# Nine gate and up pairs by seven block products, and activations split at the down projection

## The chip, the cores and the metric

The kernel runs on one NeuronCore of a Trainium2 chip. The metric is the device time of one execution in microseconds. TensorE (PE; its weight loads are PEld), VectorE (DVE), ScalarE (ACT) and GpSimd (POOL) each work off their own instructions in order; SyncE (SP) issues the DMAs. They wait for one another through semaphores.

## The reference

One block of a hybrid network on 512 tokens of width 1024 in float32: an SSD branch and a dilated attention branch are merged, and a feed-forward with a causal convolution follows. The change touches the last part:

```python
x = x + merged @ w_out[l]
h2 = rms_norm(x, norm2_g[l])
u = causal_dwconv(h2 @ w_up[l], ffn_conv_w[l], ffn_conv_b[l])   # 3 taps over tokens
u_gate, u_val = jnp.split(u, 2, axis=-1)                        # 2816 columns each
x = x + (jax.nn.silu(u_gate) * u_val) @ w_down[l]
```

## The kernel before

**Numbers.** Every matrix product is made of three matmuls: an operand `a` is split into `ahi` (a cast to fp32r, on ACT) and `alo` (`a - ahi`, on DVE), and `hi*hi + hi*lo + lo*hi` is summed in PSUM. `make_piece` (L100, L101) does so for each weight piece of 128 x 1024 elements (512 KB) that `load_piece` (L88, SP) brings; raw pieces have three buffers, their `whi` and `wlo` three each. `stt` (L52) is a helper for DVE's `scalar_tensor_tensor`.

**End of the merge.** `mm_tok` (L902) multiplies the merged activations by `w_out`, four 128-token blocks in four PSUM banks, two halves of 512 output columns (`ps_wo`). `add_x1` (L931, L933) adds the residual into `x1` in SBUF. Then the second norm: `second_norm` (L201, and `pow` on POOL in L202), `second_scale` (L52, tile `hn`), `second_t` (four transposes per half on PE, L208, and the cast `h2h` on ACT, L211), and the subtraction `h2l` on DVE (L212). Their order on DVE and ACT is written out by hand. The first gate and up pair is woven into it: its matmuls take 256 tokens at a time, so that they can begin while the last two token blocks are still normed.

**Feed-forward.** The 22 blocks `m` of 128 columns each have a gate and an up column block, together a pair. `mm_chan` (L140) makes 24 matmuls of 512 tokens for each of the two (8 slices of the width, 3 combinations). `conv3` reads the PSUM bank: ACT starts the sum (L1001), DVE adds two shifted taps (L52, tile `facc`). Gate: silu on ACT (L1022). Up: product on DVE (L1025), then the split for the down projection (L1026 on ACT, L1027 on DVE) into `act_h`, `act_l`, which stay in SBUF.

**Down projection.** `mm_tok` again (`ps_wd`), two halves of 512 columns, 11 pieces each; a piece is 24 matmuls of 512 columns. `store` adds `x1` and writes the output.

What orders DVE, ACT and POOL from the feed-forward on is the tile scheduler; PE's order is that of the code.

Of the kernel before, what the change touches and what calls it, by code (L numbers as in the profile page):

```python
# [38 lines left out]
def kernel(  # L39
# [856 lines left out]
    def mm_tok(xh, xl, nk, name, fin, last):
        pss = [bank("mm", f"ps_{name}{b}") for b in range(NT)]

        def part(b, k0, w):
            for j, (ww, xx) in enumerate(((w[0], xh), (w[0], xl), (w[1], xh))):  # L900
                for k in range(2):
                    nc.tensor.matmul(pss[b], xx[:, k0 + k, b * P:(b + 1) * P], ww[:, k, :],  # L902
                                     start=(k0 == 0 and j == 0 and k == 0),
                                     stop=(k0 == nk - 2 and j == 2 and k == 1))
# [43 lines left out]
    def second_t(b):  # L948
        for half in range(2):
            rest2[b, half] = transpose_half(hn2[b], b, half, "h", h2h, h2l)  # L950

    mm_tok(mh, ml, KD, "wo0_", lambda b, ps: add_x1(0, b, ps), 1)
    ending = mm_tok(mh, ml, KD, "wo1_", None, 2)
    with tc.manual_schedule(engines={mybir.EngineType.DVE, mybir.EngineType.Activation}):
        prefetch(1)
        add_x1(1, 0, ending(0))
        second_norm(0)
        second_scale(0, 0)
        add_x1(1, 1, ending(1))
        second_scale(0, 1)  # L960
        second_norm(1)
        second_scale(1, 0)
        ps = ending(2)
        second_t(0)
        add_x1(1, 2, ps)
        second_scale(1, 1)
        second_norm(2)
        rest2[0, 0]()
        rest2[0, 1]()
        second_scale(2, 0)  # L970
        ps = ending(3)
        second_t(1)
        add_x1(1, 3, ps)
        second_scale(2, 1)
        rest2[1, 0]()
        rest2[1, 1]()
        second_norm(3)
        up0 = [bank("mm", f"ps_u0_{i}") for i in range(2)]
        wu = [next_piece()]
        mm_chan(up0[0], wu[0], h2h, h2l, nt=256, ticks=False, lo_first=True)  # L980
        second_scale(3, 0)
        second_scale(3, 1)
        second_t(2)
        wu.append(next_piece(0))
        rest2[2, 0]()
        rest2[2, 1]()
        mm_chan(up0[1], wu[1], h2h, h2l, nt=256, ticks=False)
        prefetch(1)
        second_t(3)
        rest2[3, 0]()  # L990
        rest2[3, 1]()
        for i in range(2):
            mm_chan(up0[i], wu[i], h2h, h2l, t0=256, nt=256, ticks=False, lo_first=True)
# [74 lines left out]
```

## Time and profile before

| what | us |
|---|---|
| device time, median of 3 runs (1229.62 to 1232.95) | 1231.42 |
| device time of the profiled execution | 1231.49 |
| its span in the profile | 1229.8 |
| first gate and up matmul | 861.81 |
| first down matmul | 1106.27 |

A page of the profile has the busy time of each engine, the chain of work that ended last (followed back from the last instruction), and groups of equal instructions. Further views are the timeline of single instructions (start, duration, engine, line, operation, output <- inputs, and in brackets the idle time before it with what ended that), and the busy time in given stretches. A timeline row with x8 merges eight instructions that follow each other.

### The profile page before, as it was taken

How to read it: one execution, taken by the hardware profiler on the slowest of the kernel's cores; microseconds unless marked ns; L12 is line 12 of the kernel's file. 1: busy time of each engine (PE TensorE's matmuls, PEld its weight loads, DVE VectorE, ACT ScalarE, POOL GpSimd, SP SyncE). 2: the span in 40 equal slices, each digit the busy share in tenths (PEclk: the TensorE clock that was granted, in tenths of full speed). 3: DMA queues.
4: the chain of work that ended last, by engine and by line, in shares of the span. 5: the costliest groups of instructions: out<-in, count | busy, mean ns of one | idle time of the engine just before them, and what ended most of it. 6: DMA issues, size and time to landing. Idle time of an engine off the chain costs nothing.

```text
span 1229.8 us, 15236 instructions
## 1 busy us (share of the span) xinstructions
PE 1219.1 (99%) x6040; PEld 1021.0 (83%) x6040; DVE 701.0 (57%) x953; ACT 556.0 (45%) x847; POOL 94.4 (8%) x75
## 2 busy tenths in 40 slices
PE   9999999999999999999999999999999999999998
PEld 7889889898888788888888888888888888888887
DVE  6345544545789887777744354654765666653322
ACT  4344555747746656465433334433544444442210
POOL 1020202120001201101011000000000000000000
PEclk9999999999999999999999999999999999999999
DMA  5423222122645644434234422342333333232330
GB/s 183 120 69 92 57 64 69 54 78 61 184 124 150 166 130 121 127 87 137 70 74 129 140 87 102 103 172 85 103 88 102 96 93 103 87 102 92 107 127 34
DMA packets 152535, 128.12 MB, mean 104 GB/s; under 512 B 10368, under 2 KB 123632, under 8 KB 151441
## 3 DMA queue, kind: packets, MB, share of 16 engines
q1 hardware_dynamic: 152465, 127.16, 35.1%
q8 instruction: 47, 0.77, 0.3%
q14 instruction: 23, 0.19, 0.1%
HBM read 124.73 MB, written 2.41 MB: 103 GB/s over the span
## 4 chain that ended last, share of the span: by engine, by line
PE 91%; ACT 4%; DVE 3%; POOL 1%; issue 1%; POOLq 0%; ACTq 0%; DVEq 0%
PE ps_u L140 20%; PE ps_ssd L140 19%; PE ps_wd L902 10%; PE ps_qk L398 9%; PE ps_gate L140 7%; PE ps_sp L875 7%; PE ps_v L398 6%; PE ps_wo L902 4%; PE ps_ap L140 2%; ACT s L521 1%; PE ps_y L723 1%; PE ps_o L728 1%; PE ps_s L502 1%; POOL qrs L202 1%; PE ps_pv L540 1%; PE ps_st L704 1%
## 5 line engine op out<-in xcount | busy, mean ns | idle before, releaser
L101 DVE TENSOR_TENSOR wlo<-raw,whi 128x1024 fp32r<-128x1024 f32 x194 | 243.3, 1255 | 338.1 <-ACT whi L100 216.2
L100 ACT CAST whi<-raw 128x1024 fp32r<-128x1024 f32 x194 | 203.2, 1048 | 316.9 <-PE ps_wd L902 79.8
L140 PE MATMUL ps_ssd<-hl,whi 128*128 128x512 f32 x384 | 103.0, 397 | 0.0
L140 PE MATMUL ps_ssd<-hh,whi 128*128 128x512 f32 x384 | 98.2, 398 | 0.0
L140 PE MATMUL ps_ssd<-hh,wlo 128*128 128x512 f32 x384 | 95.3, 390 | 0.0
L140 PE MATMUL ps_u<-h2h,whi 128*128 128x512 f32 (+1 forms) x368 | 88.7, 383 | 0.3 <-ACT h2h L211 0.2
L140 PE MATMUL ps_u<-h2h,wlo 128*128 128x512 f32 (+1 forms) x368 | 88.1, 382 | 0.0
L140 PE MATMUL ps_u<-h2l,whi 128*128 128x512 f32 (+1 forms) x368 | 88.0, 382 | 0.0
L140 PEld LDWEIGHTS ps_ssd<-hh,wlo 128*128 128x128 f32 x384 | 72.1, 188 | 15.8
L140 PEld LDWEIGHTS ps_ssd<-hh,whi 128*128 128x128 f32 x384 | 70.9, 188 | 14.3
L140 PEld LDWEIGHTS ps_ssd<-hl,whi 128*128 128x128 f32 x384 | 70.1, 188 | 13.7 <-issue 0.6
L140 PEld LDWEIGHTS ps_u<-h2h,whi 128*128 128x128 f32 x368 | 67.2, 188 | 14.5 <-ACT h2h L211 0.8
L140 PEld LDWEIGHTS ps_u<-h2l,whi 128*128 128x128 f32 x368 | 67.2, 188 | 13.9
L140 PEld LDWEIGHTS ps_u<-h2h,wlo 128*128 128x128 f32 x368 | 67.2, 188 | 13.6
L52 DVE SCALAR_TENSOR_TENSOR facc<-ps_u,sc,facc 128x511 f32<-128x511 f32 x88 | 65.8, 747 | 5.8 <-ACT facc L1001 4.3
L398 PE MATMUL ps_qk<-whi,hh 128*128 128x512 f32 x192 | 66.9, 430 | 0.0
L398 PE MATMUL ps_qk<-whi,hl 128*128 128x512 f32 x192 | 60.3, 395 | 0.0
L398 PE MATMUL ps_qk<-wlo,hh 128*128 128x512 f32 x192 | 60.1, 395 | 0.0
L202 POOL TENSOR_TENSOR qrs<-qss,nhalf 128x8 f32<-128x8 f32 x24 | 44.0, 1833 | 170.7 <-DVE qss L201 170.7
L902 PE MATMUL ps_wd<-wlo,acth 128*128 128x512 f32 x176 | 54.3, 389 | 0.0
L902 PE MATMUL ps_wd<-whi,acth 128*128 128x512 f32 x176 | 54.2, 389 | 0.0
L902 PE MATMUL ps_wd<-whi,actl 128*128 128x512 f32 x176 | 54.2, 389 | 0.0
(238 smaller groups left out, 2057.9 us busy)
## 6 DMA issues: line engine op xcount, KB each, us to landing
raw<-in_w_in_dram SPq DMA_DIRECT2D x100, 512.0 KB
raw<-in_w_up_dram SPq DMA_DIRECT2D x44, 512.0 KB
raw<-in_w_down_dram SPq DMA_DIRECT2D x22, 512.0 KB
bc<-scr_a SPq DMA_DIRECT2D x8, 1024.0 KB
raw<-in_w_ssd_proj_dram SPq DMA_DIRECT2D x16, 512.0 KB
eb<-scr_e SPq DMA_DIRECT2D x16, 256.0 KB
raw<-in_w_out_dram SPq DMA_DIRECT2D x8, 512.0 KB
fb<-scr_f SPq DMA_DIRECT2D x24, 128.0 KB
```

What stands on the lines that cost most here:

```text
L52: nc.vector.scalar_tensor_tensor(o, a, s, b, op0=op0, op1=op1)
L100: nc.scalar.copy(hi, raw)
L101: nc.vector.tensor_sub(lo, raw, hi.bitcast(F32))
L140: nc.tensor.matmul(ps[:, t0:t0 + nt], a[:, k, c:c + n], b[:, k, t0:t0 + nt], start=(i == 0), stop=(i == total - 1))
L202: return nc.gpsimd.tensor_tensor(rs, ss, nhalf.broadcast_to(tuple(ss.shape)) if ss.shape[1] > 1 else nhalf, op=ALU.pow)
L398: nc.tensor.matmul(pss[b], tok(g, kq * 2 + k, b, xx), w[:, k, :], start=(kq == 0 and j == 0 and k == 0), stop=(kq == 3 and j == 2 and k == 1))
L502: nc.tensor.matmul(pss[h][:, o:o + nk * P], qt[hp, j, q * P:(q + 1) * P], kt[hp, j, (q - nk + 1) * P:(q + 1) * P], start=True, stop=True)
L521: nc.scalar.activation(s[:, o:o + nk * P], s[:, o:o + nk * P], AF.Exp, bias=st[:, q, 0, 2 * j + h:2 * j + h + 1], accum_out=st[:, q, 1, 2 ...
L540: nc.tensor.matmul(pso[h * 64:(h + 1) * 64, q * P:(q + 1) * P], vt[:, q - nk + 1 + kb, (2 * j + h) * 64:(2 * j + h + 1) * 64], pts[h][:, o ...
L704: nc.tensor.matmul(sts[c], btok[:, c, :], xdc[:, c].rearrange("p h d -> p (h d)"), start=True, stop=True)
L875: nc.tensor.matmul(pss[j], w[:, k, cs], ys[k][xi], start=(k2 == 0 and i == 0 and k == 0), stop=(k2 == 7 and i == 2 and k == 1))
L902: nc.tensor.matmul(pss[b], xx[:, k0 + k, b * P:(b + 1) * P], ww[:, k, :], start=(k0 == 0 and j == 0 and k == 0), stop=(k0 == nk - 2 and j ...
```

## The change

**Seven products for nine pairs.** The pairs 3, 5, ..., 19 are `fast`; the other 13 are taken as before. A fast pair regards the weights as a 2 x 2 block matrix (lower and upper half of the width; gate and up) and the activations as another (halves of the width; halves of the tokens), and forms the product with seven block products instead of eight, in Winograd's form of Strassen's algorithm. A block product is 12 matmuls of 256 tokens: 4 slices of the half width, 3 combinations.

- The sums of activations, S1 to S4 (each 128 x 1024), are made once, in the course of the first two pairs, on POOL and DVE, in space that `act` needs only later, and are split into `sh` and `sl`.
- The sums of weights, `t12` and `t34` (`form` 1 to 4, each 128 x 512), are made per fast pair on POOL. Such a pair then has three weight pieces to split and a half one (`w1`, `w2`, `w3`, `wb`) instead of two.
- The seven products land in four PSUM banks and are added on ACT and DVE (`sum_1`, `sum_2`, `sum_u`, `sum_g`) into `ua` and `ga` in SBUF, which the convolution reads.

**Order.** DVE, ACT and POOL have an order by hand through the whole feed-forward: the convolution of a pair runs beside the matmuls of the next one, and its weights are split one pair ahead.

**Activations are split later.** `act` stays in float32 (44 KB per partition). The down projection splits each block when it gets there (`ahead`, tiles `asp`, ten buffers), for each of its two halves anew; blocks 0 and 1 are split in the last pair. `x1` is written to DRAM after the second norm (`x1d`) and read again (`x1b`) for the final sum.

```diff
-    def mm_tok(xh, xl, nk, name, fin, last):
+    def mm_tok(xs, nk, name, fin, last, ahead=lambda k: None):
...
                 if b == 1:
+                    ahead(k0 + 2)
                     prefetch()
         ws = [next_piece(0) for i in range(last)]
+        for i in range(1, last):
+            ahead(nk - 2 * last + 2 * i)
...
+        if nh == 1:
+            nc.sync.dma_start(x1d[b * P:(b + 1) * P, :], x1[:, b, :])
...
+    PLAIN = (0, 1, *range(2, NF, 2), NF - 1)
...
+    def f_early():
+        nc.gpsimd.tensor_add(f11, h2h[quad(0, 0)].bitcast(F32), h2l[quad(0, 0)].bitcast(F32))
+        nc.gpsimd.tensor_add(f12, h2h[quad(1, 0)].bitcast(F32), h2l[quad(1, 0)].bitcast(F32))
...
+    def f_late(b):
+        for half, f in enumerate((f21, f22)):
+            nc.scalar.copy(f[:, :, (b - 2) * P:(b - 1) * P], tr2[b, half])
...
+        if which == 1:
+            nc.gpsimd.tensor_sub(w["t12"][lo_half(0)], u[lo_half(0)], g[lo_half(0)])
+        elif which == 2:
+            nc.gpsimd.tensor_sub(w["t12"][lo_half(1)], u[lo_half(1)], w["t12"][lo_half(0)])
+        elif which == 3:
+            nc.gpsimd.tensor_sub(w["t34"][lo_half(0)], u[lo_half(1)], u[lo_half(0)])
+        else:
+            nc.gpsimd.tensor_sub(w["t34"][lo_half(1)], g[lo_half(1)], w["t12"][lo_half(1)])
...
+    PRODUCTS = (("1", 0, "A11", "a", 0), ("1", 1, "A12", "c", 0), ("2", 0, "S1", "b", 1), ("2", 1, "S2", "a", 1),
+                ("3", 0, "S3", "b", 0), ("3", 1, "A22", "c", 1), ("b", 0, "S4", "d", 0))
...
+    def product(m, x, half, xo, bk, c):
...
+        for a, b in ((wh, xh), (wh, xl), (wl, xh)):
+            for k in range(4):
+                nc.tensor.matmul(ba[m][bk][:, c * H:(c + 1) * H], a[:, k, :], b[:, k, :],
+                                 start=(i == 0), stop=(i == 11))
...
+    def sum_1(m):
+        if fast(m):
+            tsum[m] = gu.tile([P, 3, H], F32, tag="ts", name=f"ts{m}", bufs=1)
+            nc.scalar.copy(tsum[m][:, 0], ba[m]["a"][:, :H])
...
+    def sum_2(m):
+        if fast(m):
+            t = tsum[m]
+            nc.vector.tensor_add(t[:, 1], t[:, 0], ba[m]["a"][:, H:])
+            nc.vector.tensor_add(t[:, 2], t[:, 1], ba[m]["b"][:, :H])
...
+            nc.vector.tensor_add(ua[m].rearrange("p (a t) -> p a t", a=2), tsum[m][:, 1:3],
+                                 ba[m]["b"][:, H:].unsqueeze(1).broadcast_to((P, 2, H)))
+            nc.vector.tensor_add(ua[m][:, :H], ua[m][:, :H], ba[m]["d"][:, :H])
...
+            nc.vector.tensor_add(ga[m].rearrange("p (a t) -> p a t", a=2), tsum[m][:, 0:3:2],
+                                 ba[m]["c"].rearrange("p (a t) -> p a t", a=2))
...
+    nc.vector.tensor_add(s1f, f21, f22)
+    nc.gpsimd.tensor_sub(s2f, s1f, f11)
+    nc.vector.tensor_sub(s3f, f11, f21)
...
+    nc.gpsimd.tensor_sub(s4f, f12, s2f)
...
+    def split_act(k, p, tag, bufs):
+        t = p.tile([P, 2, S], F32R, tag=tag, name=f"{tag}{len(asp)}_{k}", bufs=bufs)
+        nc.scalar.copy(t[:, 0, :], act[:, k, :])
+        nc.vector.tensor_sub(t[:, 1, :], act[:, k, :], t[:, 0, :].bitcast(F32))
+        return t
...
+        if fast(m):
+            steps[0]()
+            conv_a(m - 1, 1)
+            rest(m, "3")
+            load_up(m + 2)
+            steps[1]()
+            conv_a(m - 1, 0)
+            conv_s(m - 1, 1)
+            steps[2]()
+            cast(m + 1, "1")
+            rest(m, "b")
+            form(m + 2, 1)
+            steps[3]()
+            rest(m + 1, "1")
+            form(m + 2, 2)
+            steps[4]()
+            cast(m + 1, "3")
+            conv_s(m - 1, 0)
+            steps[5]()
+            silu_g(m - 1)
+            rest(m + 1, "3")
+            steps[6]()
+            mul(m - 1)
+            continue
...
+    mm_tok(xs_a, NF, "wd0_", store(0), 2, ahead)
+    ahead(0)
+    mm_tok(xs_a, NF, "wd1_", store(1), 2, ahead)
```

**The same in the instructions.** DVE in the middle of the feed-forward, before: one pair, the remainders of its two weight pieces, the convolution from PSUM (`ps_u`), the product and the split of the result.

```order
L101 TENSOR_TENSOR wlo141_7359<-raw141_7356,whi141_7358 128x1024
L52 SCALAR_TENSOR_TENSOR facc5_0_7339<-ps_u5_0_7307,sc_85,facc5_0_7339 128x511
L52 SCALAR_TENSOR_TENSOR facc5_0_7339<-ps_u5_0_7307,sc_85,facc5_0_7339 128x510
L101 TENSOR_TENSOR wlo142_7398<-raw142_7395,whi142_7397 128x1024
L52 SCALAR_TENSOR_TENSOR facc5_1_7374<-ps_u5_1_7308,sc_85,facc5_1_7374 128x511
L52 SCALAR_TENSOR_TENSOR facc5_1_7374<-ps_u5_1_7308,sc_85,facc5_1_7374 128x510
L1025 TENSOR_TENSOR facc5_1_7374<-facc5_1_7374,facc5_0_7339 128x512
L1027 TENSOR_TENSOR actl_6992<-facc5_1_7374,acth_6991 128x512
```

DVE there after the change, from the sums of the fast pair 11 (`ps_ua` to `ps_ud` are its four banks) to its product; `ulo1` and `ulo2` are remainders of pair 13.

```order
L1085 TENSOR_TENSOR ts11_8129<-ts11_8129,ps_ua11_8001 128x256
L1086 TENSOR_TENSOR ts11_8129<-ts11_8129,ps_ub11_8002 128x256
L1091 TENSOR_TENSOR ua11_8133<-ts11_8129,ps_ub11_8002 128x512
L1093 TENSOR_TENSOR ua11_8133<-ua11_8133,ps_ud11_8004 128x256
L1098 TENSOR_TENSOR ga11_8145<-ts11_8129,ps_uc11_8003 128x512
L1054 TENSOR_TENSOR ulo1_13_8143<-rawup13_0_8019,uhi1_13_8142 128x1024
L52 SCALAR_TENSOR_TENSOR act_6506<-ua11_8133,sc_85,act_6506 128x511
L52 SCALAR_TENSOR_TENSOR act_6506<-ua11_8133,sc_85,act_6506 128x510
L1054 TENSOR_TENSOR ulo2_13_8167<-t12_13_8055,uhi2_13_8166 128x1024
L52 SCALAR_TENSOR_TENSOR facc11_8162<-ga11_8145,sc_85,facc11_8162 128x511
L52 SCALAR_TENSOR_TENSOR facc11_8162<-ga11_8145,sc_85,facc11_8162 128x510
L1122 TENSOR_TENSOR act_6506<-act_6506,facc11_8162 128x512
```

The sums are new and read PSUM; a fast pair's convolution now reads two SBUF tiles, and the split of the result is gone from here.

POOL from the second norm to the first fast pair, after the change (before, the four `rs2` rows are the last on this engine):

```order
L203 TENSOR_TENSOR rs2_2_6806<-ss2_2_6805,nhalf_77 128x1
L203 TENSOR_TENSOR rs2_3_6855<-ss2_3_6854,nhalf_77 128x1
L993 TENSOR_TENSOR act_6506<-h2h_6510,h2l_6511 128x1024
L994 TENSOR_TENSOR act_6506<-h2h_6510,h2l_6511 128x1024
L1188 TENSOR_TENSOR act_6506<-act_6506 128x1024
L1193 TENSOR_TENSOR act_6506<-act_6506 128x1024
L1025 TENSOR_TENSOR t12_3_7106<-rawup3_1_7098,rawup3_0_7096 128x512
```

Four sums of 1024 columns come behind the last `pow`, and then four rows of 512 columns for each fast pair.

ACT at the end of the feed-forward, before (`whi172` to `whi182` are the pieces of the down projection's first half, `facc21` is the last pair):

```order
L100 CAST whi174_8583<-raw174_8581 128x1024
L1001 ACTIVATE facc21_1_8558<-ps_u21_1_8492,sc_85 128x512
L1026 CAST acth_6991<-facc21_1_8558 128x512
L100 CAST whi175_8613<-raw175_8611 128x1024
L100 CAST whi176_8643<-raw176_8641 128x1024
```

ACT there after the change:

```order
L101 CAST whi174_9120<-raw174_9118 128x1024
L1106 ACTIVATE act_6506<-ps_u21_1_9001,sc_85 128x512
L1106 ACTIVATE facc21_9078<-ps_u21_0_9000,sc_85 128x512
L1118 ACTIVATE facc21_9078<-facc21_9078 128x512
L101 CAST whi175_9156<-raw175_9154 128x1024
L1225 CAST asp2_2_9112<-act_6506 128x512
L1225 CAST asp3_3_9115<-act_6506 128x512
```

The casts of the activations for the second piece of the down projection, `asp2` and `asp3`, stand behind `whi175`, the fourth weight piece.

More of the change, by code (lines that the diff above doesn't have):

```diff
@@ L946, in second_scale, with second_t @@
         stt(hn2[b][:, c], x1[:, b, c], rs2[b], gb2[:, c], ALU.mult, ALU.mult)
-    def second_t(b):
+    tr2 = {}
+    def second_t(b, tag="tr"):
         for half in range(2):
[L950 to L993, printed above, removed]
@@ L1008 @@
[L1008 to L1027 removed]
+            ps = bank(tag, f"tr_h{b}_{half}")
@@ new lines, in source, with has, cast @@
+    def source(m, x):
+        w = W[m]
+        return {"1": w["g"], "2": w.get("t12"), "3": w.get("t34", w["u"]), "b": w["u"][lo_half(1)]}[x]
+    def has(m, x):
+        return fast(m) or (m < NF and x in "13")
+    def cast(m, x):
+        if not has(m, x):
+            return
+        src = source(m, x)
+        p, tag, n = {"1": (wp, "w", 3), "3": (wp, "w", 3), "2": (wx, "x", 2), "b": (wx, "b", 1)}[x]
+        hi = p.tile(list(src.shape), F32R, tag=tag + "hi", name=f"uhi{x}_{m}", bufs=n)
+        lo = p.tile(list(src.shape), F32R, tag=tag + "lo", name=f"ulo{x}_{m}", bufs=n)
+        nc.scalar.copy(hi, src)
+        W[m]["w" + x] = hi, lo
@@ new lines @@
+    f_early()
+    up0 = [bank("mm", f"ps_u0_{i}") for i in range(2)]
+    wu = [next_piece()]
+    mm_chan(up0[0], wu[0], h2h, h2l, nt=256, ticks=False, lo_first=True)
+    second_scale(3, 0)
+    second_scale(3, 1)
+    second_t(2)
+    wu.append(next_piece(0))
+    second_l(2)
+    mm_chan(up0[1], wu[1], h2h, h2l, nt=256, ticks=False)
+    prefetch(1)
+    second_t(3, "aux")
+    second_l(3)
+    x1_cm.__exit__(None, None, None)
+    wx_cm = pool("wx")
+    wx = wx_cm.__enter__()
+    gu_cm = pool("gu")
@@ new lines @@
+    low()
+    nc.gpsimd.tensor_sub(s4f, f12, s2f)
+    split_s(2, s3f)()
+    load_up(2)
+    up1 = [bank("mm", f"ps_u1_{i}") for i in range(2)]
+    mm_chan(up1[0], next_piece(0), h2h, h2l, ticks=False)
+    conv_a(0, 0)
+    conv_a(0, 1)
+    conv_s(0, 0)
+    silu_g(0)
+    conv_s(0, 1)
+    mul(0)
+    cast(2, "1")
+    low = split_s(1, s2f)
+    rest(2, "1")
+    low()
+    mm_chan(up1[1], next_piece(0), h2h, h2l, ticks=False)
+    load_up(3)
+    ga[1], ua[1] = up1
+    cast(2, "3")
+    rest(2, "3")
@@ new lines @@
+    split_s(3, s4f)()
+    form(3, 1)
+    form(3, 2)
+    ops.update({"A11": (h2h[quad(0, 0)], h2l[quad(0, 0)]), "A12": (h2h[quad(1, 0)], h2l[quad(1, 0)]),
+                "A22": (h2h[quad(1, 1)], h2l[quad(1, 1)])})
+    for i in range(4):
+        ops[f"S{i + 1}"] = sh[:, i], sl[:, i]
+    asp = {}
+    def split_act(k, p, tag, bufs):
[3 more added lines that the diff above has]
+        return t
```

256 lines of the change are left out of this document (213 added, 43 removed).

## The prediction

> **What bounds the kernel now.** I read the page's busy shares first, then the chain of work that ended last from 830 us on, then the busy time in 50 us stretches.
>
> ```profile
> span 1229.8 us, 15236 instructions
> PE 1219.1 (99%) x6040; PEld 1021.0 (83%) x6040; DVE 701.0 (57%) x953; ACT 556.0 (45%) x847; POOL 94.4 (8%) x75
> ```
> ```profile
> 861.81 3.14 PE ps_u L140 x24
> ...
> 865.83 2.83 PE ps_u L140 x24
> ...
> 869.77 236.66 PE ps_u L140 x1056
> 1106.43 119.71 PE ps_wd L902 x528
> ```
> ```profile
> 900.00:950.00 50.00, 50.00 (x220) 41.04 (x220) 31.10 (x38) 21.61 (x28) 0.00 (x0) 1.00 0.34 96
> ```
>
> TensorE is busy for 99% of the span, and from 861.81 us on the chain is nearly all matmuls: 356 us of gate and up (`ps_u`) and down projection (`ps_wd`). In a stretch of the gate and up work (columns: PE, PEld, DVE, ACT, POOL, clock, DMA share, GB/s) DVE is busy for 31.10 of 50 us, POOL for nothing, the granted clock is 1.00 and DMA is at 0.34. So a matmul saved counts fully, as long as DVE and the single waits at the edges stay covered. The profiled execution took 1231.49 us, 1.7 more than its span, and the median of the three runs is 1231.42: I sum against 1231.5 and read the result against the median.
>
> **The matmuls.** A plain pair is 48 matmuls of 512 columns, a fast pair 7 products of 12 matmuls of 256 columns, 84 in all. The 256-column form exists already in the first pair; the starts of its weight loads, eight to a row in the timeline, give its pace.
>
> ```profile
> 862.86 0.98 PEld L140 LDWEIGHTS ps_u<-h2h,wlo 128*128 128x128 f32 x8
> ...
> 863.77 0.98 PEld L140 LDWEIGHTS ps_u<-h2l,whi 128*128 128x128 f32 x8
> ...
> 866.49 1.01 PEld L140 LDWEIGHTS ps_u<-h2l,whi 128*128 128x128 f32 x8
> ...
> 867.44 1.01 PEld L140 LDWEIGHTS ps_u<-h2h,wlo 128*128 128x128 f32 x8
> ...
> 870.72 1.01 PEld L140 LDWEIGHTS ps_u<-h2h,wlo 128*128 128x128 f32 x8
> ...
> 871.66 0.42 PEld L140 LDWEIGHTS ps_u<-h2l,whi 128*128 128x128 f32 x3
> ```
>
> From 862.86 to 863.77 eight take 0.91 us, 114 ns each; from 866.49 to 867.44 0.95 us, 119 ns; from 870.72 to 871.66 0.94 us, 117.5 ns. I take 117.5. For 512 columns the chain's 236.66 us hold 48 narrow ones (5.6 us) and 1008 wide ones: 229 ns. A plain pair is 48 x 229 = 10.99 us, a fast one 84 x 117.5 = 9.87 us (9.58 to 10.0 at the ends). Nine times 1.12 is **-10.1 us** (9.0 to 12.7).
>
> [...]
>
> **VectorE and the port that it shares with GpSimd.** These are the rows of the groups (mean ns of one behind the busy time), from 860 us on, and one of the whole span.
>
> ```profile
> L101 DVE TENSOR_TENSOR wlo<-raw,whi 128x1024 fp32r<-128x1024 f32 x65 | 79.7, 1226 | 142.8 <-ACT whi L100 72.0 <-PE ps_u L140 70.8
> L100 ACT CAST whi<-raw 128x1024 fp32r<-128x1024 f32 x65 | 68.2, 1048 | 84.5 <-PE ps_wd L902 79.8 <-PE ps_u L140 4.7
> ...
> L1001 ACT ACTIVATE facc<-ps_u,sc 128x512 f32<-128x512 f32 x44 | 34.3, 779 | 28.6 <-PE ps_u L140 28.6
> ...
> L52 DVE SCALAR_TENSOR_TENSOR facc<-ps_u,sc,facc 128x510 f32<-128x510 f32 x44 | 33.0, 749 | 1.5
> ...
> L1025 DVE TENSOR_TENSOR facc<-facc,facc 128x512 f32<-128x512 f32 x22 | 15.2, 691 | 0.7
> L1022 ACT ACTIVATE facc<-facc 128x512 f32<-128x512 f32 x22 | 13.9, 632 | 42.8 <-DVE facc L52 42.8
> L1026 ACT CAST acth<-facc 128x512 fp32r<-128x512 f32 x22 | 13.6, 620 | 56.8 <-DVE facc L1025 56.8
> ```
> ```profile
> L711 DVE TENSOR_TENSOR prev<-prev,cdec 128x256 f32<-128x256 f32 x16 | 6.8, 423 | 0.4
> ```
>
> A period is now one plain and one fast pair: 10.99 + 9.87 = 20.86 us of matmuls. In it DVE has five weight remainders (5 x 1.23), one of half size (0.69), eight steps of the convolution (8 x 0.75), two products (2 x 0.69) and the fast pair's sums (three of 256 columns and two of 512: 3 x 0.42 + 2 x 0.69): 16.8 us. Before, two pairs cost it 4 x 1.23 + 8 x 0.75 + 4 x 0.69 = 13.7 of 22.0 us, 62%, which the 31.10 of 50 confirms; now it is 81%. ACT has five casts and a half one (5.9), four convolution starts (3.1), two silus (1.3) and a copy of 256 columns (at most 0.6): 10.9 us, 52%. Both lie beside the matmuls. What is new is GpSimd with four subtractions of 512 columns per fast pair. The timeline shows what such work meets:
>
> ```profile
> 450.96 2.23 DVE L101 TENSOR_TENSOR wlo<-raw,whi 128x1024 fp32r<-128x1024 f32 x1 [0.95 <-PE ps_ssd L140]
> ```
> ```profile
> 450.82 1.29 POOL L737 TENSOR_TENSOR sq<-sq 128x512 f32<-128x512 f32 x1 [23.61 <-ACT sq L734]
> ```
> ```profile
> 370.01 0.67 DVE L695 TENSOR_TENSOR xdt<-ps_xt,dtt 128x512 f32<-128x512 f32 x1
> ```
> ```profile
> 369.13 1.51 POOL L741 TENSOR_TENSOR sr<-sq,sr 128x512 fp32r<-128x512 f32 x1 [0.73 <-ACT sr L740]
> ```
> ```profile
> 406.89 6.19 POOL L737 TENSOR_TENSOR sq<-sq 128x512 f32<-128x512 f32 x1 [12.20 <-ACT sq L734]
> ```
> ```profile
> 406.70 0.69 DVE L608 TENSOR_TENSOR ysb<-ysb 128x512 f32<-128x512 f32 x1
> ...
> 409.64 2.29 DVE L664 TENSOR_TENSOR bc<-acs,bc 128x2048 f32<-128x2048 f32 x1
> ```
>
> A remainder that starts 0.14 us behind a GpSimd operation takes 2.23 us, not 1.23: two SBUF operands wait until GpSimd is done, 1.0 us lost. An operation with one operand in PSUM beside it takes its usual 0.67. The other way round, GpSimd's 1.3 us became 6.19 behind four such DVE operations in a row, which end at 411.93. In a period the plain pair's convolution (4 x 0.75) and the sums (2.6) read PSUM, 5.6 us, and 4.1 us are idle; the four subtractions need 5.2 us. Were all four to collide at 1.0 us, DVE would stand at 20.8 of 20.86. I take **0** in the loop, with the ends 0 and +10 (below).
>
> **The entry.** The first two operations of `f_early` (L993, L994; 1024 columns) stand on GpSimd right behind the last `pow` (L202), at the place where TensorE waits today:
>
> ```profile
> 864.47 1.47 POOL L202 TENSOR_TENSOR rs<-ss,nhalf 128x1 f32<-128x1 f32 x1 [4.03 <-DVE ss L201]
> ...
> 865.98 1.42 DVE L52 SCALAR_TENSOR_TENSOR hn<-x,rs,gb 128x512 f32<-128x512 f32 x2 [0.44 <-POOL rs L202]
> ...
> 867.32 1.28 DVE L212 TENSOR_TENSOR h2l<-tr_h,h2h 128x512 fp32r<-128x512 f32 x2
> ...
> 868.50 1.03 PE L208 MATMUL tr_h<-ident,hn 128*128 128x128 f32 x8
> 868.51 1.22 DVE L101 TENSOR_TENSOR wlo<-raw,whi 128x1024 fp32r<-128x1024 f32 x1
> ```
> ```profile
> 658.06 1.02 POOL L753 TENSOR_TENSOR rv<-rv,nhalf 128x4 f32<-128x4 f32 x1 [13.42 <-DMA rv<-scr_v]
> 659.04 1.20 POOL L823 COPY gt<-bct_gate 128x1024 f32<-128x1024 f32 x1
> ```
> ```profile
> L299 POOL TENSOR_TENSOR wd<-ysb,wd 128x256 fp32r<-128x256 f32 x1 | 0.7, 747 | 0.1
> ```
>
> With 0.75 us at 256 columns and 1.29 at 512, 1024 make about 2.4 us (an estimate from these two rows). GpSimd starts what stands behind as its predecessor ends (659.04 against 659.08); `hn` needs 0.04 us for the semaphore (865.94 to 865.98). So the first sum most likely takes the port, and `hn` runs from 868.3 to 869.7, where the transposes began at 868.50: 1.2 us. The second sum gets in beside the PSUM subtractions `h2l` (869.7 to 871.0) and holds the remainder behind them until 872.1; the last `h2l`, which the third eight of the matmuls need, come about 1 us late. Together 2.2 us; if `hn` wins, 0.1. I take **+2.0** (0 to 3). What follows there (copies of the transposes, S1 to S4, two more GpSimd sums) has two plain pairs, 22 us, to hide in.
>
> **The exit.** Activations are now cast when the down projection reaches them. On ACT the first cast, `asp2`, stands behind `whi175`, which waits for the buffer of the first down piece. That wait is there today:
>
> ```profile
> 1106.27 0.62 PE L902 MATMUL ps_wd<-whi,acth 128*128 128x512 f32 x2
> ...
> 1111.47 1.05 ACT L100 CAST whi<-raw 128x1024 fp32r<-128x1024 f32 x1 [0.89 <-PE ps_wd L902]
> ```
>
> Counted from the first down matmul, `whi175` runs from 5.2 to 6.25, `asp2` and `asp3` (0.62 each) to 7.49; on DVE `wlo175` to 7.48 and the two remainders (0.69) to 8.86. TensorE ends the first piece at 24 x 227 = 5.45 and wants the fourth of these operands at 6.13: **+2.7 us** (2 to 3.5). `conv_s`, `silu` and `mul` of the last pair are over by then (0.78 + 4 x 0.75 + 0.63, 4.5 us). After that a piece lasts 5.45 us and asks DVE for 1.23 + 2 x 0.69 and ACT for 1.05 + 2 x 0.62: hidden, though it happens twice. The 2 MB that `x1` writes and reads again lie in a DMA share of 0.34: nothing.
>
> **Sum:** 1231.5 - 10.1 + 2.0 + 2.7 = **1226.1 us**.
>
> **The rivals.**
> 1. *The best case*: 114 ns throughout (-12.7) and `hn` wins: 1231.5 - 12.7 + 0.1 + 2.7 = 1221.6; the first row of loads speaks for it, the two others against. Chance 0.15 for 1218 to 1222.
> 2. *Edges dearer*: bank hand-offs, or S2 and S4 starved as in the 6.19 us row, eat about 4 us more: 1230. Chance 0.12 for 1229 to 1234.
> 3. *VectorE becomes the bound* (slower). If every subtraction costs DVE its whole 1.29 us, a period asks for 16.8 + 5.2 = 22.0 us against 20.86: nine times 1.1 is 10 us, 1236. It decides from 1.0 us per collision on. For it: 81% busy and one GpSimd stream through all of it. Against: the port is free for 9.7 us a period, and a subtraction's result is wanted only a pair later. Chance 0.12 for 1234 to 1242.
> 4. *Narrow matmuls cost more when groups are short* (slower). The first group of 24 in the chain took 3.14 us, 131 ns each with its wait; at that pace a fast pair is 84 x 131 = 11.0 us, nothing is gained, and 1236 remains. It decides at 131 ns. Against it is the group at 865.83 with 118 ns. Chance 0.06.
>
> **How the numbers follow.** The forecast has 0.55 for 1222 to 1229. A measurement can tell some 0.3%, 3.7 us, from no change: faster means below 1227.7, slower above 1235.1. Faster: 0.15 + about 0.40 of the forecast's 0.55 = 0.55. Slower: most of rivals 3 and 4, 0.17. Within: the rest, 0.28. The range goes from rival 1's lower part to rivals 3 and 4: 1219.5 to 1236.5.
>
> **What would show it.** In the profile after: 256-column loads of the products 117 ns apart; fast pairs 9.9 us and plain ones 11.0 us apart with no idle TensorE between; DVE near 80% there; TensorE idle about 2 us around 868 to 874 and behind the first down piece, on `asp2` and `asp3`. Wrong would be a TensorE that waits for `ulo` or `uhi` in the loop, DVE above 95%, or remainders of 2.2 us there by the dozen.

## The result, and the profile after

| | before | after |
|---|---|---|
| device time, median of 9 runs each | 1231.36 us | 1234.46 us |
| lowest and highest | 1229.46, 1232.95 | 1232.70, 1235.75 |
| profiled execution (its span) | 1231.49 (1229.8) | 1234.85 (1233.1) |

The ratio of after to before is 1.003, 95% interval 1.0021 to 1.0038: the change costs 3.1 us where 5.3 us of gain were forecast. The page of after, busy time of the engines:

```profile
span 1233.1 us, 16094 instructions
PE 1219.4 (99%) x6364; PEld 1031.5 (84%) x6364; DVE 775.1 (63%) x1044; ACT 584.8 (47%) x904; POOL 159.6 (13%) x115
```

TensorE is as busy as before, 1219.4 us against 1219.1, although 9 x 48 matmuls of 512 columns became 9 x 84 of 256. So what they saved was given back inside TensorE's own stream and at its edges. The chain of waits of after (start, length, engine, tile, line, count):

```profile
864.06 0.59 DVE hn L52
864.65 2.23 issue
866.88 2.83 DVE hn L52
...
879.54 4.56 DVE sl L1182 x2
884.10 0.67 DVE facc L52
...
887.45 1.04 ACT uhi L1048
888.54 11.27 PE ps_u L1248 x48
```
```profile
923.84 1.45 PE ps_ub L1070 x12
...
929.58 1.45 PE ps_ud L1070 x12
931.02 11.20 PE ps_u L1248 x48
942.23 1.41 PE ps_ua L1070 x12
```
```profile
1101.92 5.04 PE ps_wd L909 x22
...
1106.98 1.06 ACT whi L101
...
1108.06 1.23 DVE wlo L102
1109.28 1.21 DVE asp L1226 x2
...
1110.54 118.71 PE ps_wd L909 x501
```

Four things are to be seen. The chain leaves TensorE at the entry (`hn`, and later `sl`, the convolution of pair 0 and `uhi` of pair 2). The 2.23 us of "issue" there are not an idle VectorE. The timeline of after has the two halves of `hn` without a break, so the first one lasts from 864.06 to 866.88, where the second starts:

```profile
864.06 5.64 DVE L52 SCALAR_TENSOR_TENSOR hn<-x,rs,gb 128x512 f32<-128x512 f32 x2 [0.44 <-POOL rs L203]
```

In the loop the chain stays on TensorE, but a plain pair takes 11.20 us where it took 10.99, with the same 48 matmuls. At the exit it runs over `whi`, `wlo` and `asp`, as the prediction said. And the down matmuls, 119.71 / 528 = 227 ns before, take 118.71 / 501 = 237 ns.

Part of that last number is the clock. Busy time in stretches of 6 us of after (PE, PEld, DVE, ACT, POOL, clock, DMA share, GB/s): behind the stall the granted clock falls (to 0.89 and 0.82 in the mean of two stretches), and 23 matmuls are counted in 6 us where 27 or 28 are at full clock.

```profile
1100.00:1106.00 6.00, 6.00 (x28) 4.91 (x27) 5.05 (x7) 2.72 (x4) 0.00 (x0) 1.00 0.36 109
1106.00:1112.00 6.00, 4.36 (x14) 2.54 (x13) 4.76 (x8) 5.66 (x10) 0.00 (x0) 0.89 0.54 173
1112.00:1118.00 6.00, 6.00 (x23) 4.78 (x22) 3.40 (x7) 2.42 (x5) 0.00 (x0) 0.82 0.70 281
```

0.11 of 6 us and 0.18 of 6 us missing at half clock make 3.5 us at half clock; the clock's own record in the trace has one stretch at 0.50, 3.41 us long, from 1110.72 on. TensorE did not stand still for all of the 3.41 us ahead of it: the longest time between the starts of two matmuls there was 1.59 us, and TensorE was busy for 1.77.

All kernels below are compared by three stretches, taken from the starts of the matmuls in the traces: *entry*, from the first matmul of pair 0 to the first of pair 2; *loop*, from there to the first down matmul; *down*, from there to the last matmul. Each ratio is to runs of before that were taken beside that kernel; their medians lay between 1230.16 and 1231.36, so two medians of this table that differ by less than about 1 us do not tell two kernels apart, and the stages decide.

| us | entry | loop | down | sum | median of runs | ratio to before (95%) |
|---|---|---|---|---|---|---|
| before | 24.72 | 219.73 | 119.47 | 363.92 | 1231.36 | |
| after | 28.65 | 213.22 | 127.09 | 368.96 | 1234.46 | 1.003 (1.0021 to 1.0038) |
| e1_exit | 28.64 | 213.22 | 122.69 | 364.54 | 1230.55 | 1.0002 (0.9992 to 1.0012) |
| e2_entry | 28.72 | 213.13 | 125.55 | 367.41 | 1234.45 | 1.0033 (1.0022 to 1.0044) |
| e3_plain | 28.69 | 219.81 | 122.83 | 371.33 | 1239.15 | 1.0073 (1.0058 to 1.0088) |
| e4_pad | 28.61 | 210.72 | 123.79 | 363.12 | 1229.14 | 0.9985 (0.9974 to 0.9996) |
| e6_before_moved | 24.88 | 217.60 | 122.97 | 365.45 | 1232.05 | 1.0015 (1.0005 to 1.0025) |
| e7_entry_held | 26.11 | 213.11 | 126.86 | 366.08 | 1232.67 | 1.0016 (1.0006 to 1.0026) |
| e8_entry_vector | 29.53 | 215.42 | 125.56 | 370.52 | 1237.19 | 1.0058 (1.0042 to 1.0074) |
| e9_pad_shift | 28.63 | 209.11 | 122.21 | 359.95 | 1227.54 | 0.9967 (0.9954 to 0.9979) |
| e10_best | 24.94 | 208.96 | 119.45 | 353.36 | 1221.01 | 0.9913 (0.9899 to 0.9926) |
| e11_best_plain | 24.96 | 217.60 | 119.45 | 362.01 | 1229.71 | 0.9985 (0.9976 to 0.9994) |
| e12_before_h2 | 24.88 | 217.60 | 119.45 | 361.93 | 1229.65 | 0.9983 (0.9973 to 0.9993) |

Between the profiles of before and after the sum grows by 5.04 us: +3.93 in the entry, -6.51 in the loop, +7.62 in the down projection. The stages ahead of the entry, whose code is the same, happened to end 1.9 us earlier in the profiled execution of after (first gate and up matmul at 859.89 against 861.81). The other profiles, too, show about the one time or the other, whatever the kernel, so stages are compared, not spans.

### The profile page after: what moved, and what is told of

It reads as the page before. It is cut to its first block, busy times and chain, and to the rows that moved or that the text cites. A ratio compares the mean times of both kernels' runs of the same rounds, so it can differ in the third digit from the quotient of the medians.

```text
span 1233.1 us, 16094 instructions
## 1 busy us (share of the span) xinstructions
PE 1219.4 (99%) x6364; PEld 1031.5 (84%) x6364; DVE 775.1 (63%) x1044; ACT 584.8 (47%) x904; POOL 159.6 (13%) x115
## 4 chain that ended last, share of the span: by engine, by line
PE 90%; DVE 4%; ACT 3%; POOL 1%; issue 1%; ACTq 0%; POOLq 0%; DVEq 0%
PE ps_ssd L141 20%; PE ps_wd L909 10%; PE ps_u L1248 10%; PE ps_qk L399 9%; PE ps_gate L141 7%; PE ps_sp L876 7%; PE ps_v L399 5%; PE ps_wo L909 3%; PE ps_ub L1070 2%; PE ps_ua L1070 2%; PE ps_uc L1070 2%; PE ps_ap L141 2%; ACT s L522 1%; PE ps_y L724 1%; PE ps_o L729 1%; PE ps_ud L1070 1%
## 5 line engine op out<-in xcount | busy, mean ns | idle before, releaser
L102 DVE TENSOR_TENSOR wlo<-raw,whi 128x1024 fp32r<-128x1024 f32 x154 | 196.2, 1276 | 254.3 <-ACT whi L101 202.0
L101 ACT CAST whi<-raw 128x1024 fp32r<-128x1024 f32 x154 | 161.4, 1049 | 302.9 <-PE ps_wd L909 64.4
L909 PE MATMUL ps_wd<-whi,asp 128*128 128x512 f32 x336 | 93.9, 400 | 1.6 <-ACT asp L1225 1.2
L909 PEld LDWEIGHTS ps_wd<-whi,asp 128*128 128x128 f32 x336 | 63.8, 190 | 18.3 <-ACT asp L1225 2.0
L909 PE MATMUL ps_wd<-wlo,asp 128*128 128x512 f32 x168 | 53.5, 400 | 0.0
L399 PEld LDWEIGHTS ps_qk<-whi,hh 128*128 128x128 f32 x192 | 46.6, 272 | 5.5 <-issue 2.7
L399 PEld LDWEIGHTS ps_qk<-whi,hl 128*128 128x128 f32 x192 | 47.0, 269 | 2.6
L399 PEld LDWEIGHTS ps_qk<-wlo,hh 128*128 128x128 f32 x192 | 47.0, 269 | 2.5
L1118 ACT ACTIVATE facc<-facc 128x512 f32<-128x512 f32 x22 | 13.9, 632 | 73.2 <-DVE facc L52 73.2
L1248 PE MATMUL ps_u<-h2h,uhi 128*128 128x512 f32 x176 | 44.7, 398 | 0.7 <-ACT uhi L1048 0.7
L1248 PE MATMUL ps_u<-h2l,uhi 128*128 128x512 f32 x176 | 44.6, 397 | 0.0
```

Source lines behind the costliest of these rows:

```text
L101: nc.scalar.copy(hi, raw)
L102: nc.vector.tensor_sub(lo, raw, hi.bitcast(F32))
L399: nc.tensor.matmul(pss[b], tok(g, kq * 2 + k, b, xx), w[:, k, :], start=(kq == 0 and j == 0 and k == 0), stop=(kq == 3 and j == 2 and k == 1))
L909: nc.tensor.matmul(pss[b], xs(k0 + k, i)[:, b * P:(b + 1) * P], ww[:, k, :], start=(k0 == 0 and j == 0 and k == 0), stop=(k0 == nk - 2 and ...
L1118: nc.scalar.activation(facc[m], facc[m], AF.Silu)
L1248: nc.tensor.matmul(pss[i], a[:, k, :], b[:, k, :], start=(n == 0), stop=(n == 23))
```

## The experiments

Two theories stood against each other for the slower matmuls: that the place of the operands in SBUF sets the pace, or that a pace is left behind by what ran before (a stall, the narrow matmuls, other engines' work). Further kernels take the entry and the exit apart. All are edits of the changed kernel, unless it is said otherwise.

**e1_exit.**

```diff
             asp[1] = split_act(1, pre, "pre", 2)
+            for k in (2, 3):
+                free = sh[:, k - 2].rearrange("p a t -> p (a t)").rearrange("p (i s) -> p i s", i=2)
+                asp[k] = split_act(k, None, None, None, free)
...
-            if i < NF:
+            if i < NF and i not in asp:
...
```

> The changed kernel, with blocks 2 and 3 of the activations split in the last pair as well (into a part of the sums' tile that is free by then), so that the down projection can take two pieces before it needs a split made behind the last pair. If the stall behind the first down piece is late splits (1.59 + 0.52 + 0.82 + 0.60 us of idle TensorE) and the half clock of 3.4 us right behind it is that stall's own consequence (1.6 us), both go: 1230.3 us, 4.2 less than the changed kernel. If the clock dip has another cause, 1231.9. If something else is late next (the weights of the next piece behind the last pair's convolutions), the stall moves back by one piece and the time stays near 1234. If the slow pace of the down matmuls (233 ns against 227) is the phase that the stall leaves behind, the down matmuls go back to 227 ns as well and the time falls by another 3.4, to 1227.

Measured: 1230.55 us, 3.9 less. The chain of waits of e1_exit:

```profile
1087.90 15.63 PE ps_u L1249 x67
1103.54 122.93 PE ps_wd L909 x528
```

The stall is gone, and with it the low clock (1.00 in e1_exit from 1101.5 to 1119.5 us). 122.93 / 528 = 233 ns remain: the pace of the down matmuls is not what the stall left behind.

**e2_entry.** `f_early()` stands behind `second_l(3)` instead of behind `second_norm(3)`.

> The changed kernel, with the two sums on GpSimd that f_early issues put behind second_l(3), so that they no longer run beside the last blocks of the second norm. If they hold the port that VectorE's scaling of hn needs (2.23 us of issue ahead of hn in the chain of waits), the idle 2.36 us of TensorE between the transposes shrinks to what before had there and the time falls by 2 to 3 us, to 1232. If the order was not the cause, no change: 1234.5. If the sums then come too late for the first fast pair, TensorE waits there and it is slower than 1234.5.

Measured: 1234.45 us, no change. But the timeline of e2_entry shows that the edit moved nothing in time:

```profile
863.43 2.40 POOL L993 TENSOR_TENSOR act<-h2h,h2l 128x1024 f32<-128x1024 f32 x1
863.49 5.64 DVE L52 SCALAR_TENSOR_TENSOR hn<-x,rs,gb 128x512 f32<-128x512 f32 x2 [0.44 <-POOL rs L203]
865.79 2.79 POOL L994 TENSOR_TENSOR act<-h2h,h2l 128x1024 f32<-128x1024 f32 x1
```

GpSimd had nothing to wait for between its `pow` and the sums, so a later place in the program left them at the same moment. The run says nothing on the theory. It says something on the clock: at the same exit stall (4.36 of 6 us busy, as in after) the granted clock stays at 1.00 in this profile.

```profile
1106.00:1112.00 6.00, 4.36 (x16) 2.60 (x15) 5.21 (x8) 5.87 (x11) 0.00 (x0) 1.00 0.63 197
```

The traces show what differs. Within a run, the clock changed only at times that lie whole multiples of 3.41 us apart (in after the starts of its stretches are 322, 1 and 35 such steps apart). In after, e4_pad and e7_entry_held one step of that grid holds most of the stall (TensorE busy for 1.77, 1.76 and 1.87 of 3.41 us), and the next step runs at half clock. In e2_entry, e8_entry_vector and e9_pad_shift an edge of the grid cuts the stall (the emptier step has 2.20, 2.19 and 2.21 us busy), and no half clock follows. So in these six profiles the same stall cost 1.7 us more or not, by where the grid fell in that execution (1.7 is an estimate, half of 3.41; the down stretches of after and e2_entry differ by 127.09 - 125.55 = 1.5). Busy time alone does not tell the cases apart: at the entry of after, a step with 1.83 us (from 868.37) was followed by full clock (1.00). In e2_entry's profile, as in those of e3_plain and e9_pad_shift, it is the entry that has a step at half clock (from 869.86). It costs nothing there, since TensorE then reaches pair 2 when `uhi` is about ready (0.24 us between the starts instead of 1.08).

**e3_plain.**

```diff
-    PLAIN = (0, 1, *range(2, NF, 2), NF - 1)
+    PLAIN = tuple(range(NF))
```

> The changed kernel with all 22 pairs taken plainly: no block products, none of their sums and splits, all else as it was changed (h2, activations and splits in their new places). Measures the nine fast pairs by themselves: by the profile they save 0.98 us each against the plain pairs of before and 1.19 against the plain pairs of the same kernel. If the plain pairs' slow pace (233 ns) comes with the fast pairs between them (a phase that they leave), all plain pairs run at 229 ns and the loop takes 8.8 - 2.2 = 6.6 us longer: 1241. If it comes from the new place of h2, they stay at 233 and it takes 10.7 us longer: 1245. The down matmuls stay at 233 ns in either case if the place of the splits sets their pace.

Measured: 1239.15 us. The chain of waits of e3_plain:

```profile
890.56 219.81 PE ps_u L1248 x960
1110.37 123.08 PE ps_wd L909 x528
```

219.81 / 960 = 229 ns: with no fast pair between them, plain pairs run as before, in the changed places. So their 233 ns in after come with the fast pairs; pair 2 of after, which has no fast pair ahead of it, goes at 228.9 ns (its last 40 spacings). The loop is 6.6 us longer than in after, as expected (-8.8 for nine pairs, +2.2 for the slower plain ones). The median is lower than the expected 1241 since in this kernel `asp2` and `asp3` happen to be cast ahead of the last silu and `whi`, and the exit stall is absent. The down matmuls stay at 233 ns.

**e4_pad.**

```diff
+    pad_cm = pool("pad", side="right")
+    pad_cm.__enter__().tile([P, 80], F32, tag="pad", name="pad")
     act_cm = pool("act", side="right")
...
```

> The changed kernel with 320 bytes of unused space per partition ahead of the activations, h2 and the down projection's splits: all right-hand tiles lie 320 bytes lower, so that they start at the same offset within 512 bytes (160) as the weights, the early splits and the sums, instead of at 480. Nothing else moves. If this offset of an operand sets the pace, the plain matmuls go from 233 to 227 ns (576 of them, -3.7 us) and the down matmuls from 233 to 227 (505, -3.4): 1227.5. If the pace is a phase that a break in the stream leaves behind, or comes from other engines' traffic, nothing changes: 1234.5.

Measured: 1229.14 us, 5.3 less. The chain of waits of e4_pad:

```profile
923.75 1.44 PE ps_ub L1072 x12
...
930.95 10.91 PE ps_u L1250 x48
...
1108.18 115.45 PE ps_wd L911 x501
```

A plain pair takes 10.91 us (227 ns) and the down matmuls go at 227 ns; the 115.45 us hold some matmuls at low clock, since the exit stall is still there. 320 unused bytes undo both slow paces. Fast pairs became a little slower (all products at 120 ns, 10.07 against 10.01 us).

**e5_offsets.** A kernel of bare streams:

```python
def block(name, mo, wo, cols, n=36, gap=True):
    ...
    for i in range(n):
        m = MV0 + mo // 4 + (i % 8) * 512
        w = WT0 + wo // 4 + (i % 8) * 128
        nc.tensor.matmul(ps[:, :cols], wt[:, w:w + P], mv[:, m:m + cols], start=(i == 0), stop=(i == n - 1))
```

> None of the reference's computation: runs of 36 fp32r matmuls, each run behind a break of a few fp32 ones, whose only difference is the byte at which the moving operand (full: 512 columns, half: 256) or the weights (wfull, whalf) start, from 0 to 480 within 512 in steps of 32 (letters a to p; f is 160, p is 480). If the start within 512 bytes sets the pace: full at f near 227 ns and at p 229 or 233, half at f near 120 and at p 113 to 118; and the same kind of difference for the weights, as the down projection showed (227 against 233). If the pace is a matter of which part of the memory the operands lie in, or of traffic beside, all sixteen agree. The pairs first and then (256 columns and behind them without a break 512, x is 160 and y is 480) tell whether a pace is handed on: then at 480 behind first at 160 would be 233 and behind first at 480 would be 229 if it is, and the same number if it is not.

Measured: the pace depends on the start of either operand, and it repeats after 256 bytes (f as n and h as p to 0.1 ns, the other letters to 1.2), so 480 counts as 224 from here on. The chain of waits of e5_offsets, 36 matmuls to a row; a row divided by 36 is up to 1.4 ns above the steady pace, for its first ones:

```profile
82.19 8.19 PE fullf L78 x36
100.56 8.26 PE fullh L78 x36
...
209.49 4.32 PE halff L78 x36
...
219.79 4.25 PE halfh L78 x36
...
330.90 8.41 PE wfullh L78 x36
...
450.33 4.10 PE whalfh L78 x36
...
514.09 8.41 PE thenxy L78 x36
...
540.96 8.26 PE thenyy L78 x36
```

The steady paces, as means of the last 24 spacings of a stream in the trace (moving start, weights start, within 256):

| ns per matmul | 160, 160 | 224, 160 | 160, 224 | 224, 224 |
|---|---|---|---|---|
| 512 columns | 226.7 | 228.9 or 233.3 | 233.3 | 226.7 |
| 256 columns | 120.0 | 117.8 | 113.3 or 117.8 (e13_handed_on) | 120.0 |

Of the eight starts of the moving operand, with weights at 160, only 160 reaches 226.7 at 512 columns, and 224 goes at 228.9; the other six lie from 232.3 to 234.5. The second value at 224, 160 is handed on: behind 256 columns at 160 and with no break the same placement goes at 233.3 (`thenxy`), behind 256 columns at 224 at 228.9 (`thenyy`). Both theories hold, each for one of the two slow paces. By the program's allocation, the down projection of after has its splits at 224 and the pieces at 160: 233. Its plain pairs have `h2` at 224 (as before) and the weights at 160, but stand behind products whose moving operands, `sh` and `sl`, start at 160: 233 in place of 229.

**e6_before_moved.** The kernel before, with 80 unused columns in a right-hand pool ahead of `x1` and `h2`, and 80 in a left-hand one ahead of `act_h` and `act_l`:

```diff
+    padr_cm = pool("padr", side="right")
+    padr_cm.__enter__().tile([P, 80], F32, tag="padr", name="padr")
...
+            padl_cm = pool("padl")
+            padl_cm.__enter__().tile([P, 80], F32, tag="padl", name="padl")
...
```

> The kernel before, with 320 unused bytes per partition ahead of h2 and 320 ahead of the activations' splits: h2 starts at 160 within 512 instead of 480, and the splits, the down projection's weights operand, at 480 instead of 160. If the place sets the pace, the gate and up matmuls go from 229 to 227 ns (1008 of them, -2.3 us) and the down matmuls from 227 to 233 or 229 (528, +3.5 or +1.2): between 1230 and 1232.7, with both paces changed in the profile. If the block products or the splits made during the down projection caused the slow paces, both stay at 229 and 227.

Measured: 1232.05 us, and both paces changed as the place says. The chain of waits of e6_before_moved:

```profile
869.78 234.53 PE ps_u L140 x1056
1104.31 123.21 PE ps_wd L904 x528
```

The first row was 236.66 us and the second 119.71 in the kernel before. No product of seven and no later split is needed for a slow down projection, only 320 bytes.

**e7_entry_held.**

```diff
     second_norm(3)
-    f_early()
...
     second_scale(3, 1)
+    held = n2.tile([P, 1], F32, tag="held", name="held")
+    nc.gpsimd.tensor_copy(held, hn2[3][:, D - 1:D])
+    f_early()
```

> The changed kernel, with f_early's two sums on GpSimd held back by a small copy that reads the end of the last block of hn, so that they cannot start before VectorE has finished it. (Put only behind it in the program's order they still ran at the same time, since nothing ahead of them on GpSimd waited.) If they held VectorE's port, the idle 2.36 us between the transposes shrinks to about 0.3 and the time falls by 2 us, to 1232.5, unless the sums now hold up the second splits of h2 or the weights of pair 1 behind it, which would give some of it back. If the gap stays at 2.36, the port is not its cause.

Measured: 1232.67 us, 1.8 less. The timeline of e7_entry_held:

```profile
864.04 1.42 DVE L52 SCALAR_TENSOR_TENSOR hn<-x,rs,gb 128x512 f32<-128x512 f32 x2 [0.44 <-POOL rs L203]
865.61 0.19 POOL L1165 COPY held<-hn 128x1 f32<-128x1 f32 x1 [1.61 <-ACT whi L101]
865.75 2.38 POOL L993 TENSOR_TENSOR act<-h2h,h2l 128x1024 f32<-128x1024 f32 x1
```

The two halves of `hn` take 1.42 us instead of 5.64: with GpSimd's sums beside them, they lost 4.2. The 2.36 us gap between the transposes is gone, and 1.4 us of the entry's loss remain, 1.1 of them in front of `uhi` of pair 2.

**e8_entry_vector.** `f_early`'s sums become `nc.vector.tensor_add` and stand behind `low()`, with `s2f` and `s3f` behind them.

> The changed kernel, with f_early's two sums on VectorE instead of GpSimd, and later, behind the low halves of the first block sum; the three sums that use them follow. If GpSimd's sums held the port, the idle 2.36 us goes as in the run before, and nothing comes back since no GpSimd work stands beside the second norm: 1232.5 or a little less. If block sums are then late, TensorE waits in front of the third or fourth product of the first fast pair, near 902 us.

Measured: 1237.19 us, slower than the changed kernel. The gap between the transposes is gone here too, but TensorE now stands for 4.7 us in front of `uhi` of pair 2. The chain of waits of e8_entry_vector:

```profile
885.20 0.76 DVE facc L52
...
887.32 0.03 ACT facc L1118
...
887.86 1.04 ACT uhi L1048
888.94 4.21 PE ps_u L1248 x9
```

VectorE reached the convolution of pair 0 later, silu (L1118) waited for it, and `uhi` stands behind silu on ScalarE. This place was expected neither here nor in the prediction. The wait brings two steps at half clock with it, from 886.94 to 893.77 us (granted clock 0.50): the nine matmuls of the last row take 468 ns each. Matmuls ran for 4.83 us of that stretch, so it cost some 2.4 us, about the 2.2 by which the loop is longer than in after.

**e9_pad_shift.** e4_pad, with the weights of the fast pairs 64 bytes later than those of the plain ones:

```diff
+            o = 16 if fast(m) else 0
+            hi, lo = (p.tile([P, 1088], F32R, tag=tag + h, name=f"u{h}{x}_{m}", bufs=n)[:, o:o + 1024].rearrange(
+                "p (a c) -> p a c", a=KD) for h in ("hi", "lo"))
...
```

> The changed kernel with the 320 bytes of the earlier run ahead of the right-hand tiles, and with the weights of the fast pairs alone started 64 bytes later than those of the plain ones (224 within 256 instead of 160). By the sweep of offsets a 256-column matmul whose moving operand starts at 160 goes at 120.0 ns with weights at 160 and at 113.3 with weights at 224. If the two starts set the pace, the 756 matmuls of the fast pairs take 5.0 us less than in the run with the 320 bytes alone, 1229.14 - 5.0 = 1224.1, and a fast pair 9.5 us. If that held only for the sweep's bare stream, 1229.

Measured: 1227.54 us, 1.6 less than e4_pad instead of 5.0. Products take 1.41 us, 117.8 ns per matmul, not 113.3.

**e10_best, e11_best_plain, e12_before_h2.** e10_best is e9_pad_shift with the edits of e1_exit and e7_entry_held, and `cast(2, "1")` ahead of `conv_s(0, 0)`. e11_best_plain is e10_best with `PLAIN = tuple(range(NF))`. e12_before_h2 is the kernel before with the right-hand 80 columns of e6_before_moved alone.

> All that the runs showed to help, together: operands placed as in the run with the shifted weights (about 1224.1), blocks 2 and 3 split in the last pair (-4.0), GpSimd's early sums held behind hn (-1.8), and the first cast of pair 2 put ahead of the activation function of pair 0 on ScalarE, so that pair 2's first matmul doesn't wait for it (1.0 to 1.3 us idle). If the parts add up, 1217.3; if exits and entries share a cover, 1219 to 1222.

> The same kernel with all 22 pairs plain: what the nine fast pairs are worth when every operand is well placed. A plain pair is then 48 matmuls at 226.7 ns, 10.88 us, and a fast one 84 at 113.3, 9.52: nine times 1.36 is 12.2 us more than the run before, 1229.5. If the additions of the fast pairs cost as much as they save, no difference.

> The kernel before with 320 unused bytes ahead of h2 alone, so that h2 starts at 160 within 256 like the weights, and the activations' splits left where they were. The gate and up matmuls go from 229 to 226.7 ns, 1008 of them: -2.3 us, 1228; if the earlier run's loss in the down projection hid no gain here, no change.

Measured: 1221.01, 1229.71 and 1229.65 us. The parts add up from what was measured: 1227.5 - 3.9 (exit) - 1.8 (hold) - 1.2 (the wait for `uhi`) is 1220.6. The lower forecast of 1217.3 contained the 113.3 ns that e9_pad_shift didn't reach. The chain of waits of e10_best has no other engine between pair 1 and the last matmul:

```profile
886.93 10.88 PE ps_u L1259 x48
897.81 1.42 PE ps_ua L1077 x12
...
907.70 10.90 PE ps_u L1259 x48
```
```profile
1095.89 119.69 PE ps_wd L911 x528
```

With all operands well placed, the nine fast pairs are worth 1229.71 - 1221.01 = 8.7 us (by the loop 8.64), and the best plain kernels, of the old form and of the new one, agree. e10_best beats the kernel before by 0.9%, and the best one with plain pairs by 0.7%.

**e13_handed_on.** Bare streams in the placement of e9_pad_shift's fast pairs (moving 160, weights 224, 256 columns), behind different ones.

> None of the reference's computation: streams of fp32r matmuls of 256 columns whose moving operand starts at 160 and whose weights start at 224 within 256, the placement of the fast pairs in the run that expected 113.3 ns and got 117.8. They run behind a break (fresh, broken), straight behind 48 matmuls of 512 columns with both operands at 160, as a fast pair stands behind a plain one (behindwide, behindagain), behind 256 columns with both at 160 (behindnarrow) and behind 512 columns in the same placement (behindshifted). If the pace of this placement depends on what ran before, fresh and broken go at 113.3 ns (84 in 9.6 us) and behindwide and behindagain at 117.8 (9.9 us). If the fast pairs were slower for another reason (other engines' reads, short groups of 12), all go at 113.3.

Measured, in the chain of waits of e13_handed_on:

```profile
47.90 9.89 PE behindwidea L78 x84
...
79.49 9.90 PE fresha L78 x84
...
116.57 9.54 PE behindshifteda L78 x84
```

Behind plain pairs' placement the stream goes at 117.8 ns, behind wide matmuls of its own placement at 113.3, and it keeps that to its end. So what ran ahead of its products is enough to explain that e9_pad_shift missed 113.3; neither other engines nor the groups of 12 are needed for it. That a break brings 113.3 back was wrong: `fresh` goes at 117.8, although in e5_offsets the same placement went at 113.3 behind the same break (`whalfh`). The break's own narrow fp32 matmuls (0.89 us in the chain) leave no idle time, so what ran ahead of it may reach across it; what a true pause does, no run shows.

## Why the prediction was wrong, point by point

**What bounds the kernel.** Right: TensorE's stream. VectorE needed 18.28 us of one period of 21.21 and 16.92 of another (86% and 80%; 81% was forecast), and TensorE was busy for all of both:

```profile
909.81:931.02 21.21, 21.21 (x133) 19.08 (x133) 18.28 (x22) 9.89 (x13) 8.23 (x7) 1.00 0.43 122
952.24:973.45 21.21, 21.21 (x133) 19.08 (x133) 16.92 (x21) 9.91 (x13) 6.25 (x5) 1.00 0.36 103
```

In the first of them two steps of the convolution beside GpSimd's subtractions took 1.78 and 1.67 us instead of 0.75, but the matmuls covered that. Of the 58 remainders in the loop two took over 2 us. The forecast of 0 for the loop's VectorE work holds, and rival 3 is false.

**The matmuls: -10.1 forecast, -6.5 measured in the loop and +3.2 outside it.** This is the step that failed. A fast pair took 10.01 us, not 9.87: products that read `sh` and `sl` go at 120 ns, those that read `h2` at 117.8. That alone, 9 x 0.98 = 8.8, would have stayed a small miss of size. The larger error was to count only the matmuls that the change replaces and to leave every other one at its pace. The plain pairs behind fast ones went from 229 to 233 ns, +2.2 us (shown by e3_plain). The down matmuls went from 227 to 233, 122.69 - 119.47 = +3.2 us between e1_exit and before, because `asp` starts at 224 within 256 where `act_h` and `act_l` started at 160 (shown by e4_pad and, from the other side, by e6_before_moved). From the forecast of -5.4 to the +5.04 of the profiles it is 10.4 us: 6.8 are this step (3.6 in the loop, 3.2 in the down projection), 1.9 the entry and 1.7 the exit.

The clue stood in the prediction's own rows. Weight loads 114, 119 and 117.5 ns apart in one place, and 229 ns in `ps_u` against 227 in `ps_wd`, were read as scatter and averaged. In the trace of before, the matmuls of the first group of 24 settle at 113.4 ns and those of the later groups at 117.8, to which the rows of 119 and 117.5 both belong; at 512 columns they go at 228.9 and 226.7. These are separate steady paces of the same instruction, and the question should have been what tells them apart.

A fast pair stayed cheaper than a plain one, by less than the 1.12 us that were counted: against plain pairs of before a fast one of after gains 0.98 us, in e4_pad 0.84 against its neighbours, in e10_best 0.96 (8.64 / 9).

**The entry: +2.0 forecast, +3.9 measured.** The mechanism was right (e7_entry_held), the course was not. The "port" of the prediction stands for measured times: beside GpSimd's sums the two halves of `hn` took 5.64 us instead of 1.42, as the remainder of the prediction's row took 2.23 instead of 1.23; what the two engines share no run shows. Each half of `hn` lost to one of the two sums: the first took 2.82 us and the second 2.83 (the timeline row and the chain of after) instead of some 0.7, since the second sum started before the second half did. That is 4.2 us on VectorE against the 1.2 that were counted for `hn`, and 2.5 us of the entry's time (28.65 - 26.11). The rest came from a sentence that failed: "What follows there ... has two plain pairs, 22 us, to hide in". On ScalarE the first cast of pair 2 stands behind silu of pair 0, that waits for the convolution on VectorE, and that stands behind the first two splits of the sums (`sl`). These met GpSimd's next two sums: the two `sl` took 4.56 us in the chain of after, where the later ones take 1.21 each, and `wlo` ahead of them 2.43 instead of 1.23, 3.3 us on VectorE that the prediction had left to the 22 us. No run has the path without them. TensorE stood 0.85 us in front of `uhi`. e10_best, with the cast ahead of the convolution, has 24.94 us there, 0.2 above before.

**The exit: +2.7 forecast, 2.6 measured as idle time** (1.59 + 0.52 + 0.82 + 0.60 us between starts, less the four matmuls' own 0.92), on the operands that were named. What the sum left out is the half clock behind it, 4.40 - 2.6 = 1.8 us in the profiled execution (4.40 is the down stretch of after less that of e1_exit). By where the clock's grid falls it can be absent from an execution, as in e2_entry's. The median's +3.1 us would fit the 5.04 without this term, +3.2, and as well the 5.04 less the 1.9 us by which earlier stages ended sooner in that execution; the record does not tell which.

**Rivals.** Rival 1 and rival 4 are false: no product at 114 ns, none at 131. Rival 2, edges that cost some 4 us more, is what the edges did (3.9 + 2.6 + 1.8 against 4.7), by other means than the bank hand-offs and the starved sums that it named. No rival had a changed pace of matmuls that the change doesn't touch, and without it the measured slower side had no mechanism.

## What to carry to other kernels

A change that moves a tile moves the start of a matmul operand, and that alone cost 3% of every matmul that read it here (the down matmuls' 119.71 us became 123.21 in e6_before_moved); after such a change compare the spacing of the matmuls that were *not* touched, and try a pad (here 320 bytes, e4_pad) before giving the idea up. Different steady paces of one instruction in the profile are a finding, not scatter to be averaged. GpSimd's sums, placed later in the order of an engine that waited for nothing, started no later (863.43 us against 863.49 for `hn` in e2_entry, 864.00 against 864.06 in after); only the dependence on `hn` held them back, to 865.75, when `hn` had ended at 865.46 (e7_entry_held).
